# 340 dense tokens, 44 in two lanes beside the last 128, and row buffers that change roles

## The chip, the core and the metric

The kernel runs on one core of a Trainium2 chip. The time is the device time of one execution in microseconds (us), the median of the runs shown. TensorE is PE in the profile (its weight loads PEld), VectorE is DVE, ScalarE is ACT, GpSimd is POOL, SyncE is SP.

## What is computed

One decoder layer on 512 tokens of 2048 channels: RMS norm, a projection into a convolution group and an attention group, their output projection added to x, and then a channel mixer (PEER) on the normed result. The mixer is what the change is about:

```python
v1, i1 = lax.top_k(sub[:, :, 0], 16)          # 8 heads, 128 keys each half
v2, i2 = lax.top_k(sub[:, :, 1], 16)
vals, cidx = lax.top_k(v1[..., :, None] + v2[..., None, :] , 16)
experts = e1 * 128 + e2                        # 128 experts for each token
gates = softmax(vals)
h = einsum("cd,chkd->chk", xc, peer_u[experts])
a = gelu(h) * gates
y = einsum("chk,chkd->cd", a, peer_v[experts])
```

There are 16384 experts, each a row of 2048 floats in `peer_u` and in `peer_v`; each token uses 128 of them.

## The kernel before

The tokens of the mixer are split in three.

- **Dense tokens**, the first `TD` = 352. All experts are run for them, and a gate that is zero for the experts not chosen is applied. `expert_tile` (L940 on) makes, for one tile of 128 experts, 48 matmuls over `TD` columns (L949, L951, L952: three products of the high and low parts of weights and tokens, 16 chunks of channels), with a Gelu behind it. `fold_group` (L987 on) makes for eight such tiles eight pieces of 48 matmuls of the same width (L998, L1000, L1001) and adds them to `acc` on DVE (L1008).
- **The last 128 tokens**, one a partition. For each of their 128 experts a row is fetched by an indirect load from POOL (L845, `gather`), and one DVE instruction multiplies and sums it (L861, first half, rows of `peer_u`) or adds it to the output rows (L878, second half, rows of `peer_v`).
- **The `NB` = 32 tokens between**, in `LANES` = 4 lanes on the same 128 partitions: each lane does a quarter of a token's experts, so `SB` = 32 further steps in each half. The four partial sums of a token are added by a matmul at the end (`yo`, L1056).

So there are `STEPS` = 2 x (128 + 32) = 320 gather steps. In the first half steps 0 to 127 are of the last tokens and 128 to 159 of the lanes, and so again in the second half. Step n is one indirect load and one DVE instruction of 2048 elements a partition. The loads go in turn to two buffers `grow` and to a third, the row tile that the half does not use (`yrow` in the first, `xrow` in the second). A buffer is free again when the DVE instruction that reads it has ended.

The weights come from SP as one load for two units (8 KB a partition); ACT makes the rounded high part `w_hi` (L152), DVE the rest `w_lo` (L153); three buffers of each let them run ahead of PE.

Order. The program issues 256 ticks of 48 matmuls: 72 of `expert_tile` (groups 0 to 8, gelu values written to DRAM), then for groups 9 to 15 eight of `expert_tile` and eight of `fold_group`, then 72 of `fold_group`. `step` (L933 on) counts them and asks for gather steps by this rule:

```python
if tick[0] > START:
    gather_until(int((tick[0] - START) * STEPS / (END - START)) + 1, first)
```

Other DVE and ACT work (the decoding of the choices, `dense_gates` for `GT` = 16 tokens a chunk with its PE matmuls at L921) stands in a queue from which each tick takes some (`pump`). The framework then sets the final order of each engine by its own estimate of times, and each engine runs its list in order; what waits on one engine holds all behind it there. Three times a row tile is loaded anew when its step is reached: `xrow` at step 128, `yrow` at 160 and again at 288.

Of the kernel before, what the change touches and what calls it, by code (L numbers as in the profile page):

```python
# [9 lines left out]
FT = mybir.dt.float32  # L10
# [50 lines left out]
def hymba_layer(ctx: ExitStack, tc: tile.TileContext, xT, pos, par, row, wi, wo, wq, sk, ut, un, vt, vn,  # L61
                out_t, out_r, dbg=None):
    nc = tc.nc
# [107 lines left out]
    ident = const.tile([128, 128], FT, name="ident")  # L171
# [82 lines left out]
    for c in range(KC):  # L254
        if c % 4 == 0:
# [5 lines left out]
                                       op1=OP.subtract)  # L261
# [48 lines left out]
    at = ctx.enter_context(ExitStack())  # L310
# [225 lines left out]
    gat = ctx.enter_context(tc.tile_pool(name="gat", bufs=1))  # L536
# [298 lines left out]
    h3 = gat.tile([128, 128 + SB], FT, name="h3")  # L835
    rows = {"x": xrow, "y": None}
    STEPS = 2 * (128 + SB)

    def gather(src, k, after):
        if done[0] % 3 < 2:  # L840
            g = pu.tile([128, D], FT, name="grow", bufs=2)
        else:
            g = gat.tile([128, D], FT, name="yrow" if src is un else "xrow", bufs=1)
        at = idx[:, k:k + 1] if k < 128 else idxb[:, k - 128:k - 127]
        i = nc.gpsimd.indirect_dma_start(out=g, out_offset=None, in_=src,  # L845
                                         in_offset=bass.IndirectOffsetOnAxis(ap=at, axis=0))
        if after is not None:
            tc.add_manual_dep(i.ins, after.ins.name,
                              mybir.DependencyInfo(mybir.DependencyClass.NoSync, mybir.DependencyReason.DATA),
                              reason="spreads the gathers over the dense sweep")  # L850
        return g

    def gather_step(n, after):
        k = n % (128 + SB)
        if n < 128 + SB:
            if k == 128:
                rows["x"] = gat.tile([128, D], FT, name="xrow", bufs=1)
                for l in range(LANES):
                    nc.scalar.dma_start(rows["x"][l * NB:l * NB + NB], XB)
            g = gather(un, k, after)  # L860
            nc.vector.scalar_tensor_tensor(g, g, 1.0, rows["x"], op0=OP.mult, op1=OP.mult, accum_out=h3[:, k:k + 1])  # L861
            if k % 16 == 15:
                s = slice(k - 15, k + 1)
                w = GA3[:, s] if k < 128 else GB3[:, k - 143:k - 127]
                nc.scalar.activation(h3[:, s], h3[:, s], AF.Gelu)
                nc.vector.tensor_tensor(h3[:, s], h3[:, s], w, op=OP.mult)
        else:
            if k == 0:
                rows["y"] = gat.tile([128, D], FT, name="yrow", bufs=1)
                nc.scalar.dma_start(rows["y"], YA)  # L870
            if k == 128:
                nc.scalar.dma_start(out_r[NB:], rows["y"])
                rows["y"] = gat.tile([128, D], FT, name="yrow", bufs=1)
                nc.gpsimd.memset(rows["y"], 0.0)
                nc.scalar.dma_start(rows["y"][:NB], YB)
            y = rows["y"]
# [238 lines left out]
```

## Time and profile before

| | us |
|---|---|
| median of 3 runs | 2865.03 |
| runs, lowest to highest | 2859.58 to 2870.8 |
| the profiled execution, its own time | 2866.89 |
| its span, first to last instruction | 2864.8 |
| mean granted TensorE clock | 0.99 of full |

The profile is one execution; times in it count from the start of its span. Busy time is the time in which an engine has an instruction running; matmuls overlap, so PE's rate is read from the starts of successive matmuls. In the timeline the number behind the start is the duration, and a bracket holds the idle time before it with what ended it.

### The profile page before, as it was taken

The numbers are of one execution on the slowest core, as the hardware profiler recorded it, in microseconds if no ns is written. First come the engines' busy times: TensorE is split into PE (matmuls) and PEld (weight loads), VectorE is DVE, ScalarE is ACT, GpSimd is POOL, SyncE is SP. The second block draws the span as 40 slices with busy tenths as digits, with TensorE's granted clock in tenths as the row PEclk, the third lists the DMA queues.
The fourth block names the chain that finished last, engine by engine and source line by source line (L and its number), as shares of the span: only waits on it lengthen the run. The fifth ranks groups of instructions, "written<-read, shape, count | busy, mean of one in ns | idle before, by whom it ended". The sixth has DMA issues, their size and how long they took to land.

```text
span 2864.8 us, 42910 instructions
## 1 busy us (share of the span) xinstructions
PE 2812.4 (98%) x16995; PEld 2693.1 (94%) x16995; DVE 2369.8 (83%) x3586; ACT 1210.9 (42%) x1879; POOL 460.1 (16%) x337
## 2 busy tenths in 40 slices
PE   8999999999999999999999999999999999999996
PEld 8998877788899999999999999999999999999995
DVE  7888996569999888878688878788888888888796
ACT  5566434343343777666333332333323333333321
POOL 0000000000002122212221222222222112222232
PEclk9999999999999999999999999999999999999998
DMA  5222322433249989999989889899898988888796
GB/s 175 74 67 75 117 91 82 165 112 136 89 153 342 325 312 354 326 340 344 357 346 345 339 323 352 336 334 339 324 345 329 354 333 336 346 317 337 278 377 240
DMA packets 167337, 763.94 MB, mean 267 GB/s; under 512 B 14496, under 2 KB 66848, under 8 KB 90784
## 3 DMA queue, kind: packets, MB, share of 16 engines
q1 hardware_dynamic: 66720, 378.64, 35.7%
q0 software_dynamic: 46080, 335.56, 31.4%
q10 hardware_dynamic: 54336, 47.00, 4.9%
q8 instruction: 133, 2.18, 0.3%
q14 instruction: 68, 0.56, 0.1%
HBM read 716.42 MB, written 44.70 MB: 266 GB/s over the span
## 4 chain that ended last, share of the span: by engine, by line
PE 95%; DVE 2%; DMA 2%; issue 1%; ACT 1%; POOL 0%; POOLq 0%; ACTq 0%; DVEq 0%
PE mm L951 11%; PE mm L949 11%; PE mm L952 11%; PE mm L1000 11%; PE mm L998 11%; PE mm L1001 11%; PE gps L921 3%; PE mm L599 2%; PE mm L600 2%; PE mm L816 2%; PE mm L818 2%; PE mm L817 2%; PE mm L511 2%; PE mm L510 2%; PE mm L509 2%; PE mm L598 2%
## 5 line engine op out<-in xcount | busy, mean ns | idle before, releaser
L152 ACT ACTIVATE w_hi<-w_raw 128x1024 fp32r<-128x1024 f32 x628 | 664.5, 1059 | 1266.7 <-PE mm L1000 618.2
L153 DVE TENSOR_TENSOR w_lo<-w_raw,w_hi 128x1024 fp32r<-128x1024 f32 x628 | 766.8, 1224 | 310.9 <-ACT w_hi L152 307.7
L951 PE MATMUL mm<-nl,w_hi 128*128 128x352 f32 x2048 | 667.5, 326 | 0.0
L949 PE MATMUL mm<-nh,w_hi 128*128 128x352 f32 x2048 | 665.8, 325 | 1.0 <-ACT w_hi L152 1.0
L952 PE MATMUL mm<-nh,w_lo 128*128 128x352 f32 x2048 | 663.5, 325 | 0.0
L1000 PE MATMUL mm<-al,w_hi 128*128 128x352 f32 x2048 | 661.3, 323 | 0.0
L998 PE MATMUL mm<-ah,w_hi 128*128 128x352 f32 x2048 | 658.7, 323 | 1.7 <-DVE acc L1008 1.7
L1001 PE MATMUL mm<-ah,w_lo 128*128 128x352 f32 x2048 | 650.0, 323 | 2.0 <-DVE w_lo L153 1.9
L998 PEld LDWEIGHTS mm<-ah,w_hi 128*128 128x128 f32 x2048 | 384.7, 188 | 2.6 <-DVE acc L1008 2.6
L949 PEld LDWEIGHTS mm<-nh,w_hi 128*128 128x128 f32 x2048 | 384.6, 188 | 1.5 <-ACT w_hi L152 1.3
L1001 PEld LDWEIGHTS mm<-ah,w_lo 128*128 128x128 f32 x2048 | 383.3, 188 | 2.6 <-DVE w_lo L153 2.6
L1000 PEld LDWEIGHTS mm<-al,w_hi 128*128 128x128 f32 x2048 | 385.3, 188 | 0.0
L952 PEld LDWEIGHTS mm<-nh,w_lo 128*128 128x128 f32 x2048 | 385.0, 188 | 0.0
L951 PEld LDWEIGHTS mm<-nl,w_hi 128*128 128x128 f32 x2048 | 384.9, 188 | 0.2
L845 POOL DMA_INDIRECT grow<-un,idx x86 | 122.0, 1419 | 889.0 <-DVE grow L861 577.7
L878 DVE SCALAR_TENSOR_TENSOR yrow<-grow,h,yrow 128x2048 f32<-128x2048 f32 x107 | 251.1, 2347 | 7.3 <-DMA grow<-vn,idxb 7.3
L861 DVE SCALAR_TENSOR_TENSOR grow<-grow,xrow 128x2048 f32<-128x2048 f32 x107 | 244.2, 2284 | 3.5 <-DMA grow<-un,idxb 3.5
L845 POOL DMA_INDIRECT grow<-vn,idx x85 | 117.4, 1381 | 453.1 <-DVE yrow L878 439.0
L306 DVE SCALAR_TENSOR_TENSOR mix_c<-h,par,mix_c 128x512 f32<-128x512 f32 x240 | 173.7, 748 | 1.6
L1008 DVE TENSOR_TENSOR acc<-acc,mm 128x352 f32<-128x352 f32 x240 | 116.9, 517 | 56.4 <-PE mm L1001 56.1
L878 DVE SCALAR_TENSOR_TENSOR yrow<-xrow,h,yrow 128x2048 f32<-128x2048 f32 x53 | 124.4, 2347 | 0.1
L861 DVE SCALAR_TENSOR_TENSOR yrow<-yrow,xrow 128x2048 f32<-128x2048 f32 x53 | 121.1, 2285 | 1.0 <-DMA xrow<-XB 1.0
(274 smaller groups left out, 3889.5 us busy)
## 6 DMA issues: line engine op xcount, KB each, us to landing
w_raw<-ut SPq DMA_DIRECT2D x128, 1024.0 KB
w_raw<-vt SPq DMA_DIRECT2D x128, 1024.0 KB
w_raw<-wi SPq DMA_DIRECT2D x52, 512.0 KB
G<-gt ACTq DMA_DIRECT2D x22, 1024.0 KB
Gb<-G SPq DMA_DIRECT2D x16, 1408.0 KB
w_raw<-wo SPq DMA_DIRECT2D x32, 512.0 KB
w_raw<-wq SPq DMA_DIRECT2D x32, 512.0 KB
H<-gl ACTq DMA_DIRECT2D x18, 704.0 KB
```

Source lines behind the costliest of these rows:

```text
L152: nc.scalar.activation(hi, raw, AF.Copy)
L153: nc.vector.tensor_tensor(lo, raw, hi.bitcast(FT), op=OP.subtract)
L306: nc.vector.scalar_tensor_tensor(mix_c[:, c], h[:, k:k + T], w, mix_c[:, c], op0=OP.mult, op1=OP.add)
L845: i = nc.gpsimd.indirect_dma_start(out=g, out_offset=None, in_=src, in_offset=bass.IndirectOffsetOnAxis(ap=at, axis=0))
L861: nc.vector.scalar_tensor_tensor(g, g, 1.0, rows["x"], op0=OP.mult, op1=OP.mult, accum_out=h3[:, k:k + 1])
L878: nc.vector.scalar_tensor_tensor(y, g, h3[:, k:k + 1], y, op0=OP.mult, op1=OP.add)
L949: m = nc.tensor.matmul(bank, hi[:, s], nh[:, k, :TD], start=k == 0, stop=False)
L951: nc.tensor.matmul(bank, hi[:, s], nl[:, k, :TD], start=False, stop=False)
L952: nc.tensor.matmul(bank, lo[:, s], nh[:, k, :TD], start=False, stop=k == KC - 1)
L998: m = nc.tensor.matmul(banks[j], hi[:, ws], ah[:, ee], start=ee == 0, stop=False)
L1000: nc.tensor.matmul(banks[j], hi[:, ws], al[:, ee], start=False, stop=False)
L1001: nc.tensor.matmul(banks[j], lo[:, ws], ah[:, ee], start=False, stop=ee == 7)
```

## The change

`TD` becomes 340 and `NB` 44. There are two lanes in place of four, so a lane step covers `PB` = 88 partitions, and there are `SB` = 64 of them in each half: `STEPS` = 2 x (128 + 64) = 384. Gate chunks hold 20 tokens in place of 16 (17 chunks in place of 22, and 85 calls of `dense_gates` in place of 88). `START` and `END` go from 10 and 250 to 2 and 249. The row tile for the next stretch is loaded three steps ahead into the buffer that was the third gather buffer; then the two names change roles. The closing matmul has 44 output rows.

```diff
-TD = 352
+TD = 340
 TA = T - 128
 NB = TA - TD
-LANES = 128 // NB
+LANES = 2
+PB = LANES * NB
 SB = 128 // LANES
-GT = 16
+GT = 20
 AHEAD = 9
-START = 10
-END = 250.0
+START = 2
+END = 249.0
...
+    def load_rows(n):
+        t = gat.tile([128, D], FT, name=home[1], bufs=1)
+        if n == 128 + SB:
+            nc.scalar.dma_start(t, YA)
+        elif n == 128:
+            for l in range(LANES):
+                nc.scalar.dma_start(t[l * NB:l * NB + NB], XB)
+        else:
+            nc.gpsimd.memset(t, 0.0)
+            nc.scalar.dma_start(t[:NB], YB)
+        spare[n] = t
...
-        if done[0] % 3 < 2:
+        if done[0] % 3 < 2 or spare:
             g = pu.tile([128, D], FT, name="grow", bufs=2)
         else:
-            g = gat.tile([128, D], FT, name="yrow" if src is un else "xrow", bufs=1)
-        at = idx[:, k:k + 1] if k < 128 else idxb[:, k - 128:k - 127]
+            g = gat.tile([128, D], FT, name=home[1], bufs=1)
+        at = idx[:, k:k + 1] if k < 128 else idxb[:PB, k - 128:k - 127]
+        g = g[:128 if k < 128 else PB]
...
+        if n + 3 in SWITCH:
+            load_rows(n + 3)
+        if n in spare:
+            if n == SWITCH[2]:
+                nc.scalar.dma_start(out_r[NB:], rows["y"])
+            rows["x" if n == 128 else "y"] = spare.pop(n)
+            home.reverse()
...
-        nc.tensor.matmul(ps, fold_s.rearrange("p l n -> p (l n)"), rows["y"][:, cs], start=True, stop=True)
+        nc.tensor.matmul(ps[:NB], fold_s, rows["y"][:, cs], start=True, stop=True)
```

How the built programs stand. First DVE in the stretch of the lane steps of the first half, near tick 102: `w_lo` is one per 24 matmuls, the instruction with `x2048` is a gather step. Before:

```order
L153 TENSOR_TENSOR w_lo<-w_raw,w_hi 128x1024 x2
L861 SCALAR_TENSOR_TENSOR grow,h_7303<-grow,xrow 128x2048
L1008 TENSOR_TENSOR acc<-acc,mm 128x352 x2
L861 SCALAR_TENSOR_TENSOR grow,h_7303<-grow,xrow 128x2048
L153 TENSOR_TENSOR w_lo<-w_raw,w_hi 128x1024 x2
L861 SCALAR_TENSOR_TENSOR yrow,h_7303<-yrow,xrow 128x2048
L1008 TENSOR_TENSOR acc<-acc,mm 128x352 x2
```

Now:

```order
L154 TENSOR_TENSOR w_lo<-w_raw,w_hi 128x1024
L884 SCALAR_TENSOR_TENSOR xrow,h_7303<-xrow,yrow 88x2048
L154 TENSOR_TENSOR w_lo<-w_raw,w_hi 128x1024
L884 SCALAR_TENSOR_TENSOR grow,h_7303<-grow,yrow 88x2048
L1024 TENSOR_TENSOR acc<-acc,mm 128x340 x2
L154 TENSOR_TENSOR w_lo<-w_raw,w_hi 128x1024
L890 TENSOR_TENSOR h_7303<-h_7303,GB_5224 88x16
L884 SCALAR_TENSOR_TENSOR grow,h_7303<-grow,yrow 88x2048
L154 TENSOR_TENSOR w_lo<-w_raw,w_hi 128x1024
L884 SCALAR_TENSOR_TENSOR xrow,h_7303<-xrow,yrow 88x2048
L1024 TENSOR_TENSOR acc<-acc,mm 128x340 x2
```

Before there are three gather steps for two ticks in this place; now each `w_lo` has a step behind it, two for each tick. Over ticks 80 to 119 DVE's list holds 54 gather steps before and 78 now. Over ticks 0 to 23 it holds 18 before and 32 now, with 9 fewer of the decoding instructions on `dec_oh` (L770 to L774) and 4 fewer `oh` of the gates, which stand later. In the other stretches up to tick 247 eight ticks hold 8 to 13 steps now and 6 to 13 before.

Then the end of DVE's list, from one of the last `w_lo` on. The two `acc` rows come after the last matmuls of `fold_group`. Before:

```order
L153 TENSOR_TENSOR w_lo<-w_raw,w_hi 128x1024
L878 SCALAR_TENSOR_TENSOR yrow<-grow,h_7303,yrow 128x2048
L153 TENSOR_TENSOR w_lo<-w_raw,w_hi 128x1024
L878 SCALAR_TENSOR_TENSOR yrow<-xrow,h_7303,yrow 128x2048
L1008 TENSOR_TENSOR acc<-acc,mm 128x352 x2
L878 SCALAR_TENSOR_TENSOR yrow<-grow,h_7303,yrow 128x2048
L1008 TENSOR_TENSOR acc<-acc,mm 128x352 x2
L878 SCALAR_TENSOR_TENSOR yrow<-grow,h_7303,yrow 128x2048
L878 SCALAR_TENSOR_TENSOR yrow<-xrow,h_7303,yrow 128x2048
L878 SCALAR_TENSOR_TENSOR yrow<-grow,h_7303,yrow 128x2048 x2
L878 SCALAR_TENSOR_TENSOR yrow<-xrow,h_7303,yrow 128x2048
L878 SCALAR_TENSOR_TENSOR yrow<-grow,h_7303,yrow 128x2048 x2
```

Now, up to the fifth step behind the last `acc`:

```order
L154 TENSOR_TENSOR w_lo<-w_raw,w_hi 128x1024
L894 SCALAR_TENSOR_TENSOR yrow<-grow,h_7303,yrow 88x2048
L154 TENSOR_TENSOR w_lo<-w_raw,w_hi 128x1024
L1024 TENSOR_TENSOR acc<-acc,mm 128x340 x2
L894 SCALAR_TENSOR_TENSOR yrow<-grow,h_7303,yrow 88x2048
L894 SCALAR_TENSOR_TENSOR yrow<-xrow,h_7303,yrow 88x2048
L1024 TENSOR_TENSOR acc<-acc,mm 128x340 x2
L894 SCALAR_TENSOR_TENSOR yrow<-grow,h_7303,yrow 88x2048 x2
L894 SCALAR_TENSOR_TENSOR yrow<-xrow,h_7303,yrow 88x2048
L894 SCALAR_TENSOR_TENSOR yrow<-grow,h_7303,yrow 88x2048 x2
L894 SCALAR_TENSOR_TENSOR yrow<-xrow,h_7303,yrow 88x2048
```

Behind the last `acc` stand 7 gather steps before. Now the pattern of the last three rows goes on to the end of the list: 30 steps, all of 88 partitions, with nothing else between them; the loads on POOL stand in the same order.

## Rows read from the trace of the kernel before

**Rows 1.** the page, parts 1, 3 and 4: busy time, DMA queues, the chain.

```profile
PE 2812.4 (98%) x16995; PEld 2693.1 (94%) x16995; DVE 2369.8 (83%) x3586; ACT 1210.9 (42%) x1879; POOL 460.1 (16%) x337
...
q0 software_dynamic: 46080, 335.56, 31.4%
...
PE 95%; DVE 2%; DMA 2%; issue 1%; ACT 1%; POOL 0%; POOLq 0%; ACTq 0%; DVEq 0%
```

**Rows 2.** busy time by stretch (us, PE, PEld, DVE, ACT, POOL, clock, DMA share, GB/s).

```profile
764.00:957.00 193.00, 192.01 (x1191) 189.61 (x1190) 183.67 (x480) 81.56 (x112) 26.57 (x18) 1.00 0.66 242
1600.00:1800.00 200.00, 200.00 (x1252) 200.00 (x1251) 162.22 (x176) 62.94 (x73) 46.96 (x35) 1.00 0.91 339
2400.00:2600.00 200.00, 200.00 (x1247) 200.00 (x1246) 174.20 (x190) 66.92 (x84) 44.53 (x29) 1.00 0.87 339
2215.00:2225.00 10.00, 10.00 (x65) 10.00 (x64) 5.89 (x7) 2.97 (x3) 0.98 (x1) 1.00 1.01 427
```

**Rows 3.** timeline of PE: first and last matmul of runs at 256, 512 columns, and gates (start, us).

```profile
201.40 0.28 PE L327 MATMUL mm<-w_hi,xh 128*128 128x256 f32 x1
...
202.72 0.28 PE L330 MATMUL mm<-w_hi,xl 128*128 128x256 f32 x1
...
699.76 0.40 PE L817 MATMUL mm<-nl,w_hi 128*128 128x512 f32 x1
...
703.03 0.39 PE L816 MATMUL mm<-nh,w_hi 128*128 128x512 f32 x1
...
951.52 1.95 PE L921 MATMUL gps<-og,oh 128*128 128x128 f32 x16
953.23 0.41 PE L949 MATMUL mm<-nh,w_hi 128*128 128x352 f32 x1
```

**Rows 4.** the page, part 5: weight loads of one dense line (count, busy, mean ns).

```profile
L998 PEld LDWEIGHTS mm<-ah,w_hi 128*128 128x128 f32 x2048 | 384.7, 188 | 2.6 <-DVE acc L1008 2.6
```

**Rows 5.** timeline of DVE near 1600 us: one gather step between its neighbours.

```profile
1599.26 2.29 DVE L861 SCALAR_TENSOR_TENSOR grow<-grow,xrow 128x2048 f32<-128x2048 f32 x1
1601.47 0.08 DVE L861 DVE_READ_ACCUMULATOR grow<-grow,xrow 128x1 f32 x1
1601.47 0.52 DVE L188 TENSOR_TENSOR al<-hv,ah 128x352 fp32r<-128x352 f32 x1
1601.90 1.22 DVE L153 TENSOR_TENSOR w_lo<-w_raw,w_hi 128x1024 fp32r<-128x1024 f32 x1
1603.04 2.29 DVE L861 SCALAR_TENSOR_TENSOR yrow<-yrow,xrow 128x2048 f32<-128x2048 f32 x1
```

**Rows 6.** groups of DVE instructions by line, 764 to 957 us (count, busy, mean ns, idle).

```profile
L153 DVE TENSOR_TENSOR w_lo<-w_raw,w_hi 128x1024 fp32r<-128x1024 f32 x49 | 60.0, 1225 | 8.4 <-ACT w_hi L152 7.6 <-issue 0.7
...
L772 DVE TENSOR_TENSOR dec_oh<-dec_oh,iif 128x1024 f32<-128x1024 f32 x10 | 12.3, 1225 | 0.0
...
L914 DVE TENSOR_TENSOR oh<-iof,kt 128x1024 f32<-128x1024 f32 x4 | 4.7, 1218 | 0.0
```

**Rows 7.** timeline: the first dense w_lo on DVE, the first sweep matmul on PE.

```profile
763.57 1.25 DVE L153 TENSOR_TENSOR w_lo<-w_raw,w_hi 128x1024 fp32r<-128x1024 f32 x1
...
772.73 0.33 PE L949 MATMUL mm<-nh,w_hi 128*128 128x352 f32 x1
```

**Rows 8.** timeline of DVE, 2737 to 2773 us: first and last of nine gather steps.

```profile
2737.09 2.35 DVE L878 SCALAR_TENSOR_TENSOR yrow<-grow,h,yrow 128x2048 f32<-128x2048 f32 x1
...
2772.47 2.35 DVE L878 SCALAR_TENSOR_TENSOR yrow<-xrow,h,yrow 128x2048 f32<-128x2048 f32 x1
```

**Rows 9.** timeline of the end: PE's last dense matmul, DVE's steps, the closing matmul.

```profile
2831.04 0.32 PE L1001 MATMUL mm<-ah,w_lo 128*128 128x352 f32 x1
...
2831.84 2.35 DVE L878 SCALAR_TENSOR_TENSOR yrow<-grow,h,yrow 128x2048 f32<-128x2048 f32 x1
2834.22 2.35 DVE L878 SCALAR_TENSOR_TENSOR yrow<-xrow,h,yrow 128x2048 f32<-128x2048 f32 x1
2836.61 2.35 DVE L878 SCALAR_TENSOR_TENSOR yrow<-grow,h,yrow 128x2048 f32<-128x2048 f32 x1
2841.96 2.35 DVE L878 SCALAR_TENSOR_TENSOR yrow<-grow,h,yrow 128x2048 f32<-128x2048 f32 x1 [3.00 <-DMA grow<-vn,idxb]
2844.39 2.35 DVE L878 SCALAR_TENSOR_TENSOR yrow<-xrow,h,yrow 128x2048 f32<-128x2048 f32 x1
2847.61 2.35 DVE L878 SCALAR_TENSOR_TENSOR yrow<-grow,h,yrow 128x2048 f32<-128x2048 f32 x1 [0.87 <-DMA grow<-vn,idxb]
2852.20 2.35 DVE L878 SCALAR_TENSOR_TENSOR yrow<-grow,h,yrow 128x2048 f32<-128x2048 f32 x1 [2.24 <-DMA grow<-vn,idxb]
...
2854.61 2.07 PE L1056 MATMUL yo<-yrow,fold_s 128*128 128x512 f32 x2 [23.25 <-DVE yrow L878]
```

**Rows 10.** timeline of POOL in that stretch: issues of indirect loads.

```profile
2834.45 2.93 POOL L845 DMA_INDIRECT grow<-vn,idxb  x1 [5.83 <-DVE yrow L878]
2837.69 2.08 POOL L845 DMA_INDIRECT xrow<-vn,idxb  x1 [0.30 <-issue]
2840.08 0.94 POOL L845 DMA_INDIRECT grow<-vn,idxb  x1 [0.31 <-issue]
2844.58 2.97 POOL L845 DMA_INDIRECT grow<-vn,idxb  x1 [3.56 <-DVE yrow L878]
```

**Rows 11.** the chain of waits, 2830 us to the end: from an issue to its landing.

```profile
2834.45 7.41 DMA grow<-vn,idxb
...
2844.58 7.53 DMA grow<-vn,idxb
```

More of the change, by code (lines that the diff above doesn't have):

```diff
@@ L667, in hymba_layer @@
             xb = xtp.tile([128, 512], FT, name="xb", bufs=1)
-            nc.scalar.activation(xb[128 - NB:], src[128 - NB:], AF.Copy)
+            nc.scalar.activation(xb[64:], src[64:], AF.Copy)
             nc.scalar.dma_start(to[:, c4 * 512:c4 * 512 + 512], xb[128 - NB:])
@@ L792, in lane_lists @@
     def lane_lists():
-        ps_ = slice(128 - NB, 128)
+        ps_ = slice(64, 128)
         ib = kp.tile([128, 128], I32, name="ib")
@@ L796, in lane_lists @@
         e2 = E2[ps_, 2].rearrange("p h k -> p (h k)")
-        ga = GA[ps_, 2].rearrange("p h k -> p (h k)")
+        ga = GA[128 - NB:, 2].rearrange("p h k -> p (h k)")
         nc.vector.scalar_tensor_tensor(ib[ps_], e1, 128.0, e2, op0=OP.mult, op1=OP.add)
         for l in range(LANES):
-            nc.scalar.dma_start(idxb[l * NB:l * NB + NB], ib[ps_, l * SB:l * SB + SB])
+            nc.scalar.dma_start(idxb[l * NB:l * NB + NB], ib[128 - NB:, l * SB:l * SB + SB])
             nc.scalar.dma_start(GB3[l * NB:l * NB + NB], ga[:, l * SB:l * SB + SB])
@@ L834, in hymba_layer @@
     pu = ctx.enter_context(tc.tile_pool(name="pu", bufs=1))
-    h3 = gat.tile([128, 128 + SB], FT, name="h3")
+    h3 = pu.tile([128, 128 + SB], FT, name="h3")
     rows = {"x": xrow, "y": None}
     STEPS = 2 * (128 + SB)
+    home = ["xrow", "yrow"]
+    spare = {}
+    def load_rows(n):
[9 more added lines that the diff above has]
+        spare[n] = t
     def gather(src, k, after):
-        if done[0] % 3 < 2:
+        if done[0] % 3 < 2 or spare:
             g = pu.tile([128, D], FT, name="grow", bufs=2)
         else:
-            g = gat.tile([128, D], FT, name="yrow" if src is un else "xrow", bufs=1)
-        at = idx[:, k:k + 1] if k < 128 else idxb[:, k - 128:k - 127]
+            g = gat.tile([128, D], FT, name=home[1], bufs=1)
+        at = idx[:, k:k + 1] if k < 128 else idxb[:PB, k - 128:k - 127]
+        g = g[:128 if k < 128 else PB]
         i = nc.gpsimd.indirect_dma_start(out=g, out_offset=None, in_=src,
@@ L851, in gather @@
         return g
+    SWITCH = (128, 128 + SB, 256 + SB)
     def gather_step(n, after):
         k = n % (128 + SB)
+        if n + 3 in SWITCH:
[5 more added lines that the diff above has]
+            home.reverse()
+        p = 128 if k < 128 else PB
         if n < 128 + SB:
[L856 to L859, printed above, removed]
             g = gather(un, k, after)
-            nc.vector.scalar_tensor_tensor(g, g, 1.0, rows["x"], op0=OP.mult, op1=OP.mult, accum_out=h3[:, k:k + 1])
+            nc.vector.scalar_tensor_tensor(g, g, 1.0, rows["x"][:p], op0=OP.mult, op1=OP.mult,
+                                           accum_out=h3[:p, k:k + 1])
             if k % 16 == 15:
                 s = slice(k - 15, k + 1)
-                w = GA3[:, s] if k < 128 else GB3[:, k - 143:k - 127]
-                nc.scalar.activation(h3[:, s], h3[:, s], AF.Gelu)
-                nc.vector.tensor_tensor(h3[:, s], h3[:, s], w, op=OP.mult)
-        else:
[L868 to L876, printed above, removed]
+                w = GA3[:, s] if k < 128 else GB3[:PB, k - 143:k - 127]
+                nc.scalar.activation(h3[:p, s], h3[:p, s], AF.Gelu)
+                nc.vector.tensor_tensor(h3[:p, s], h3[:p, s], w, op=OP.mult)
+        else:
+            y = rows["y"][:p]
             g = gather(vn, k, after)
-            nc.vector.scalar_tensor_tensor(y, g, h3[:, k:k + 1], y, op0=OP.mult, op1=OP.add)
+            nc.vector.scalar_tensor_tensor(y, g, h3[:p, k:k + 1], y, op0=OP.mult, op1=OP.add)
     done = [0]
@@ L1045, in hymba_layer @@
     gather_until(STEPS, None)
-    fold_s = mg.tile([128, LANES, NB], FT, name="fold_s")
-    nc.vector.tensor_copy(fold_s[:, 0], ident[:, 0:NB])
+    fold_s = mg.tile([128, NB], FT, name="fold_s")
+    nc.vector.tensor_copy(fold_s, ident[:, 0:NB])
     for l in range(1, LANES):
-        nc.vector.tensor_tensor(fold_s[:, 0], fold_s[:, 0], ident[:, l * NB:l * NB + NB], op=OP.add)
-    for l in range(1, LANES):
-        nc.vector.tensor_copy(fold_s[:, l], fold_s[:, 0])
+        nc.vector.tensor_tensor(fold_s, fold_s, ident[:, l * NB:l * NB + NB], op=OP.add)
     yo = pu.tile([128, D], FT, name="grow", bufs=2)
```

## The prediction

> **What bounds the kernel now.** I read the page first: PE is busy for 98% of the span and makes 95% of the chain of waits [rows 1]. So nearly all time is a count of matmuls times their spacing. The stretches say it more finely: in the 200 us from 1600 us on PE starts 1252 matmuls at the full clock and is never idle, while DVE is busy for 162 us and the DMA engines for 0.91 [rows 2]. One dense matmul of 352 columns thus costs 200 / 1252 = 159.7 ns. Two other things must be kept in mind: DVE is close behind PE (184 of 193 us at the start of the sweep, 174 of 200 late in the folds [rows 2]), and after the last dense matmul PE stops and the rest is a tail of gather steps, 2831.4 to 2854.6 us, with 10 us of closing work behind it [rows 9]. The change makes PE's part shorter, gives DVE more, and alters the tail, so each is priced by itself.
>
> **Matmuls of 340 columns.** There are 12288 of them (256 ticks of 48). Spacing at other widths shows what a column costs: at 256 columns 11 starts take 1.32 us, 120 ns each; at 512 columns 14 starts take 3.27 us, 233.6 ns each [rows 3]. From 256 to 352 that is 39.7 ns for 96 columns, 0.41 ns each; from 352 to 512 it is 73.9 for 160, 0.46 each. Twelve columns fewer save 5.0 to 5.5 ns; I take 5.25, so 12288 x 5.25 ns = 64.5 us (61 to 68). The new spacing is 154.4 ns. [...]
>
> **Gates.** Three calls of `dense_gates` fewer are 24 matmul records fewer; 16 of them take 1.71 us from their first start to the next dense one [rows 3], so 24 save 2.6 us. ACT and DVE work of these calls is beside PE and counts nothing.
>
> **The start of the sweep.** DVE's list has 14 more gather steps in the first 24 ticks, 9 fewer on `dec_oh` and 4 fewer `oh`. A step takes 2.21 us to the next instruction's start [rows 5], so +31 us; the others 1.22 us each [rows 6], less some overlap, so -15. DVE was busy for 184 of 193 us there [rows 2] and would need 200, where PE needs 24 x 48 x 154.4 ns = 178 in place of 184. DVE starts 9 us ahead of PE [rows 7], so PE waits for some 22 - 9 = 13 us, against a few before. I take 11 us more (4 to 20).
>
> **The lane steps of the first half.** Ticks 80 to 119 hold 78 steps, where it were 54. In these 40 ticks DVE has 80 `w_lo` at 1.14 us from start to start, 78 steps at 2.21 and 80 small ones (`hv`, `al` or `acc`) at 0.43 [rows 5]: 91 + 172 + 34 = 298 us; PE needs 40 x 48 x 154.4 ns = 296.5. DVE is thus as long as PE, with no room for what it waits for. Nothing, if it packs perfectly; the other end is the pace of steps beside the dense stream late in the kernel, eight in 35.4 us or 4.42 each [rows 8], which for 78 is 345 us, 48 too many, though with loads of 128 rows and not 88. I take 6 us. Elsewhere the list holds 8 to 13 steps for eight ticks, much as before, and DVE keeps its room; I cost the full-width steps there at nothing, hidden behind PE. If that cover went, each late step would hold the `w_lo` behind it.
>
> **The switches.** Three loads of row tiles go out three steps earlier; the chain before holds none of them, so I count nothing. During the three steps the third gather buffer is missing, six to nine steps in all, beside PE. [...]
>
> **The tail.** This term decides. DVE runs its list in order, and behind the last `acc`, which waits for the last matmul, stand 30 steps where it were 7. Before, the 7 took 23.2 us, from 2831.4 to 2854.6 [rows 9]: three found their rows landed and ran 2.39 us apart, then each buffer went round in 10.1 to 10.2 us (2831.84 to 2841.96 to 2852.20), so three steps in 10.2, 3.4 each. The round can be followed [rows 9 to 11]: the step ends; POOL issues the next load into its buffer, 2.93 us because DVE is at the next step meanwhile (0.94 us where DVE was idle); the load lands 7.4 us after the issue began; the step of 2.35 us. With rows of 88 partitions DVE's step is as long (2048 elements a partition). Only the load may shrink: 320 loads hold 31.4% of the 16 engines' span [rows 1], 2.81 us each, of which 40 of 128 rows are 0.88. A round is then 9.3 us, 3.1 a step. If all three loads were always in time, DVE alone would set 2.39; if a load of 88 rows takes as long as one of 128, 3.4. No row shows how 88 rows spread, so I take 3.2, nearest to the measured round: 30 x 3.2 = 96 us, 73 more than before (49 at 2.39, 79 at 3.4). The closing work is as before.
>
> **Sum.** On the profiled execution, 2866.9: -64.5 - 2.6 + 11 + 6 + 73 = 2889.8. That execution is 1.9 above the median, so I forecast 2888 us: slower by 0.8%. The columns gain what was to be gained, and the tail gives back a little more than that. 0.5% is about what a measurement of this kernel can tell from no change.
>
> **Rivals.**
>
> - *The load of 88 rows is no shorter than one of 128.* [...] No run here shows a gather of 88. As a mechanism: the round stays 10.2 us, a step 3.4, the tail 102 us, the time 2894. It would show as loads of the same time from first issue to landing. Against it stands nothing in the rows. Chance 0.18.
> - *No change.* The tail at 3.0 (90 us, +67) and DVE keeping up at the start and in the lanes: 2866.9 - 67 + 67 - 1.9 = 2865. For it: DVE has idle time in most stretches and PE's stalls were few. Against it: the sums for DVE above exceed PE's. Values from 2851 to 2879 fall here. Chance 0.25.
> - *Faster: DVE sets the tail.* If POOL's issues fall into gaps of DVE (0.94 us in place of 2.93, 2 us less a round) and 88 rows land 0.9 us sooner, a round is 7.3 us and the steps come 2.4 us apart, 72 us in all, +49. With 68 us from the columns and no new stalls: 2866.9 - 68 - 2.6 + 49 - 1.9 = 2843. It decides from a round below 7.2 us on, three DVE steps. Against it: the three issues that met a step took 2.08 to 2.97 us, and only the one made while DVE was idle took 0.94 [rows 10]. Chance 0.10.
> - *Slower by more: lane steps hold PE.* If the 78 steps run at 4.42 us, 48 us in place of 6: 2930. For it: beside the dense stream the loads were only just in time [rows 8]; against it: fewer bytes a load. Chance 0.10.
> - *The columns don't count, since weight loads set the spacing.* A load shows 188 ns [rows 4], more than the spacing. Then nothing is gained and the time is 2952. Against it: with the same loads 256 columns go at 120 ns [rows 3]. Chance 0.03.
>
> DMA engines as the bound: 64 more steps of 88 rows but two lanes mean 256 x 1.05 + 128 x 0.72 = 361 MB of gathers in place of 336; 22 of it falls in the tail. The dense part, 3% shorter, would move some 350 GB/s, below the 427 that ten microseconds show [rows 2]. I hold this in the range, not as a case.
>
> **How the numbers follow.** The forecast has 0.34 and lies from 2880 to 2905 by its bounds. With the first rival (0.18), the lanes (0.10) and the weight loads (0.03) slower by over 0.5%, above 2879, has 0.65; no change 0.25; faster 0.10. The range takes the upper half of the no-change case and part of the lanes' rival: 2856 to 2914, leaving out about 0.1 on either side.
>
> **What would show it.** Dense matmuls 154 to 155 ns apart. The last dense matmul near 2781 us (2831 - 67 + 17). Thirty steps behind it, 9.3 to 10.2 us a round, POOL issues near 3 us where they meet a step. DVE near 100% at 800 to 950 us and in ticks 80 to 119, with PE idle there for 10 to 25 us. I am wrong if the tail's steps come 2.4 us apart, if PE shows no idle time before the tail, or if the spacing stays at 160 ns.

## The result and the profile after

The change made the kernel slower: 3117.38 us (median of 4 runs, 3110.0 to 3120.02) beside 2865.04 us before (4 runs, 2859.58 to 2870.8), a ratio of 1.0877 with a 95% interval of 1.0853 to 1.0901. The forecast was 2888 us, with a range up to 2914: the sign was right, the size was 23 us in place of 252.

The page of the changed kernel, parts 1, 3 and 4, beside [rows 1]:

```profile
PE 2801.1 (90%) x16971; PEld 2664.7 (85%) x16971; DVE 2501.7 (80%) x3676; ACT 1211.0 (39%) x1866; POOL 618.3 (20%) x401
...
q0 software_dynamic: 55296, 360.76, 36.1%
q1 hardware_dynamic: 66727, 377.41, 35.1%
...
PE 67%; issue 14%; DMA 9%; DVE 6%; POOL 3%; ACT 1%; POOLq 0%; DVEq 0%
```

PE was the bound before (95% of the chain of waits); now it makes 67%. The gather queue q0 moves 7.5% more bytes, and its packets take 36.1% x 3116.7 = 1125 us of the 16 engines where it were 31.4% x 2864.8 = 900, 25% more. The weights, on q1, moved the same bytes within 0.4% and took 1094 us where it were 1023 (35.7% of the span before).

Busy time by stretch in the changed kernel (columns as in [rows 2]):

```profile
764.00:957.00 193.00, 185.85 (x1186) 182.76 (x1185) 191.39 (x435) 73.76 (x91) 53.14 (x33) 1.00 0.85 320
...
1600.00:1800.00 200.00, 140.76 (x768) 135.85 (x768) 124.32 (x131) 40.60 (x50) 62.05 (x32) 0.85 0.95 212
2000.00:2200.00 200.00, 200.00 (x1294) 200.00 (x1293) 165.71 (x142) 69.64 (x84) 41.59 (x35) 1.00 0.88 335
2400.00:2600.00 200.00, 198.43 (x1279) 197.87 (x1278) 176.52 (x194) 65.21 (x78) 50.52 (x30) 1.00 0.90 343
```

Where the loads fetch 128 rows (2000 to 2200 us) all is as forecast: PE never idle, 200 / 1294 = 154.6 ns from matmul to matmul, 335 GB/s with the DMA engines 0.88 busy. In the lane stretch (1600 to 1800 us) PE starts 768 matmuls in place of some 1290, DVE is less busy than elsewhere, and the DMA engines are 0.95 busy but move only 212 GB/s. Neither PE nor DVE is the limit there; the engines that carry the loads are full and slow.

The timeline of DVE in that stretch of the changed kernel shows how this reaches PE:

```profile
1655.32 2.29 DVE L884 SCALAR_TENSOR_TENSOR xrow<-xrow,yrow 88x2048 f32<-88x2048 f32 x1 [2.37 <-DMA xrow<-un,idxb]
...
1657.54 1.22 DVE L154 TENSOR_TENSOR w_lo<-w_raw,w_hi 128x1024 fp32r<-128x1024 f32 x1
1667.08 2.29 DVE L884 SCALAR_TENSOR_TENSOR grow<-grow,yrow 88x2048 f32<-88x2048 f32 x1 [8.32 <-DMA grow<-un,idxb]
```

A lane step waits 8.32 us for its load, and everything behind it on DVE waits too: the next `acc` and `w_lo`, and behind these PE. The groups of waits of the changed kernel (us in total, times, longest):

```profile
DVE grow L884 <- DMA grow<-un,idxb: 94.3, 31, 8.3
DVE yrow L894 <- DMA grow<-vn,idxb: 76.0, 30, 6.0
...
PE mm L1017 <- DVE w_lo L154: 60.0, 27, 6.6
PE mm L968 <- DVE w_lo L154: 43.4, 17, 7.4
PE mm L1014 <- DVE acc L1024: 33.9, 11, 6.7
```

Before, the corresponding waits for lane loads came to 3.5 us (first half) and 7.3 us (second half).

The tail of the changed kernel (timeline of all engines), beside [rows 9 to 11]:

```profile
2979.89 2.35 DVE L894 SCALAR_TENSOR_TENSOR yrow<-xrow,h,yrow 88x2048 f32<-88x2048 f32 x1 [5.86 <-DMA xrow<-vn,idxb]
...
2982.53 0.96 POOL L862 DMA_INDIRECT xrow<-vn,idxb  x1 [6.38 <-DVE yrow L894]
...
2990.43 2.35 DVE L894 SCALAR_TENSOR_TENSOR yrow<-xrow,h,yrow 88x2048 f32<-88x2048 f32 x1 [0.29 <-DMA xrow<-vn,idxb]
...
3102.92 2.35 DVE L894 SCALAR_TENSOR_TENSOR yrow<-xrow,h,yrow 88x2048 f32<-88x2048 f32 x1 [0.79 <-DMA xrow<-vn,idxb]
...
3105.37 6.05 PE L1070 MATMUL yo<-yrow,fold_s 128*44 128x512 f32 x8 [129.64 <-issue]
```

31 steps stand between the last dense matmul and the end, 2979.89 to 3102.92: 4.10 us a step, where the forecast took 3.2 and allowed 3.4. (The first of them stands ahead of the last `acc` in DVE's list, so the 30 of the forecast are the others.) The load issued at 2982.53 landed 7.9 us later although its issue took only 0.96; before, 7.41 us held an issue of 2.93 [rows 10, 11]. Behind the issue this load takes 6.9 us, where the one before took 4.5.

### The profile page after: what moved, and what is told of

It reads as the page before. It is cut to its first block, busy times and chain, and to the rows that moved or that the text cites. A ratio compares the mean times of both kernels' runs of the same rounds, so it can differ in the third digit from the quotient of the medians.

```text
span 3116.7 us, 43134 instructions
## 1 busy us (share of the span) xinstructions
PE 2801.1 (90%) x16971; PEld 2664.7 (85%) x16971; DVE 2501.7 (80%) x3676; ACT 1211.0 (39%) x1866; POOL 618.3 (20%) x401
## 3 DMA queue, kind: packets, MB, share of 16 engines
q0 software_dynamic: 55296, 360.76, 36.1%
## 4 chain that ended last, share of the span: by engine, by line
PE 67%; issue 14%; DMA 9%; DVE 6%; POOL 3%; ACT 1%; POOLq 0%; DVEq 0%
PE mm L965 7%; PE mm L968 7%; PE mm L967 7%; PE mm L1017 6%; PE mm L1014 6%; PE mm L1016 6%; DMA grow<-vn,idxb 3%; PE gps L937 2%; POOL grow L862 2%; PE mm L600 2%; PE mm L817 2%; PE mm L512 2%; PE mm L511 2%; PE mm L818 2%; PE mm L819 2%
## 5 line engine op out<-in xcount | busy, mean ns | idle before, releaser
L1017 PE MATMUL mm<-ah,w_lo 128*128 128x340 f32 x2048 | 647.9, 326 | 60.0 <-DVE w_lo L154 60.0
L968 PE MATMUL mm<-nh,w_lo 128*128 128x340 f32 x2048 | 655.5, 322 | 43.5 <-DVE w_lo L154 43.4
L1014 PE MATMUL mm<-ah,w_hi 128*128 128x340 f32 x2048 | 661.6, 325 | 33.9 <-DVE acc L1024 33.9
L965 PE MATMUL mm<-nh,w_hi 128*128 128x340 f32 x2048 | 660.1, 322 | 14.5 <-DVE acc L1024 11.5
L1016 PE MATMUL mm<-al,w_hi 128*128 128x340 f32 x2048 | 660.8, 323 | 9.9 <-DVE al L189 9.9
L967 PE MATMUL mm<-nl,w_hi 128*128 128x340 f32 x2048 | 659.0, 322 | 0.0
L894 DVE SCALAR_TENSOR_TENSOR xrow<-grow,h,xrow 128x2048 f32<-128x2048 f32 x87 | 204.3, 2349 | 1.6 <-DMA grow<-vn,idx 1.6
L884 DVE SCALAR_TENSOR_TENSOR grow<-grow,yrow 88x2048 f32<-88x2048 f32 x43 | 98.3, 2286 | 94.5 <-DMA grow<-un,idxb 94.3
L894 DVE SCALAR_TENSOR_TENSOR yrow<-grow,h,yrow 88x2048 f32<-88x2048 f32 x42 | 98.6, 2347 | 76.1 <-DMA grow<-vn,idxb 76.0
L1024 DVE TENSOR_TENSOR acc<-acc,mm 128x340 f32<-128x340 f32 x240 | 113.3, 504 | 47.6 <-PE mm L1017 47.4
```

Source lines behind the costliest of these rows:

```text
L884: nc.vector.scalar_tensor_tensor(g, g, 1.0, rows["x"][:p], op0=OP.mult, op1=OP.mult, accum_out=h3[:p, k:k + 1])
L894: nc.vector.scalar_tensor_tensor(y, g, h3[:p, k:k + 1], y, op0=OP.mult, op1=OP.add)
L965: m = nc.tensor.matmul(bank, hi[:, s], nh[:, k, :TD], start=k == 0, stop=False)
L967: nc.tensor.matmul(bank, hi[:, s], nl[:, k, :TD], start=False, stop=False)
L968: nc.tensor.matmul(bank, lo[:, s], nh[:, k, :TD], start=False, stop=k == KC - 1)
L1014: m = nc.tensor.matmul(banks[j], hi[:, ws], ah[:, ee], start=ee == 0, stop=False)
```

## Where the 252 us are

The dense stream has 256 ticks of 48 matmuls, so the starts of certain matmuls (first of the stream, of ticks 80, 128 and 240, and the last) cut every run into the same stretches. Timeline of PE before (first and last are in [rows 7, 9]):

```profile
1471.43 0.32 PE L998 MATMUL mm<-ah,w_hi 128*128 128x352 f32 x1
...
1842.34 0.33 PE L998 MATMUL mm<-ah,w_hi 128*128 128x352 f32 x1
...
2707.97 0.33 PE L998 MATMUL mm<-ah,w_hi 128*128 128x352 f32 x1
```

The same of the changed kernel:

```profile
764.83 0.32 PE L965 MATMUL mm<-nh,w_hi 128*128 128x340 f32 x1
...
1447.23 0.32 PE L1014 MATMUL mm<-ah,w_hi 128*128 128x340 f32 x1
...
1964.48 0.32 PE L1014 MATMUL mm<-ah,w_hi 128*128 128x340 f32 x1
...
2810.93 0.32 PE L1014 MATMUL mm<-ah,w_hi 128*128 128x340 f32 x1
...
2975.41 0.31 PE L1017 MATMUL mm<-ah,w_lo 128*128 128x340 f32 x1
```

And of the run `e9_after_64_mid` (below), which is the changed kernel with other lane loads:

```profile
769.07 0.32 PE L969 MATMUL mm<-nh,w_hi 128*128 128x340 f32 x1
...
1453.12 0.32 PE L1018 MATMUL mm<-ah,w_hi 128*128 128x340 f32 x1
...
1845.69 0.32 PE L1018 MATMUL mm<-ah,w_hi 128*128 128x340 f32 x1
...
2691.38 0.32 PE L1018 MATMUL mm<-ah,w_hi 128*128 128x340 f32 x1
...
2810.33 0.31 PE L1021 MATMUL mm<-ah,w_lo 128*128 128x340 f32 x1
```

Fewer columns take 48 x (159.74 - 154.56) ns = 0.249 us off a tick, 63.7 us in all. What is left of the differences to before, with that taken out by itself:

| stretch | after, us | e9, us | forecast, us |
|---|---|---|---|
| up to the first dense matmul | -7.9 | -3.7 | 0 |
| 12 columns fewer, all ticks | -63.7 | -63.7 | -64.5 |
| ticks 0 to 79 (start of the sweep, gates) | +3.6 | +5.3 | +8.4 |
| ticks 80 to 127 (lanes, first half) | +158.3 | +33.6 | +6 |
| ticks 128 to 239 | +8.7 | +7.9 | 0 |
| ticks 240 to 255 (lanes, second half) | +45.4 | -0.1 | 0 |
| behind the last dense matmul | +107.5 | +59.1 | +73 |
| sum, against the span of 2864.8 | +251.9 | +38.4 | +22.9 |

So little was lost where the gathers have 128 rows (at most 8.7 us in a stretch, and 7.9 of it in e9 too). Nearly all of the surprise lies in the three stretches with loads of 88 rows.

## The experiments

Runs e1 to e6, e9 and e10 are single executions; the others have five or six.

**Is it the loads, and what about them?** The first four runs shared a chip, on which the kernel before took 2862.49 us. The theories then: the number of rows decides (88 does not divide over 16 engines as 80, 96 and 128 do); the pace of 192 steps in a half is too high whatever the rows; any load that covers a part of the 128 partitions is slow.

`e1_rows96`: the changed kernel, lane loads of 96 rows (8 of them unused).

```diff
+GP = 96
...
-        at = idx[:, k:k + 1] if k < 128 else idxb[:PB, k - 128:k - 127]
+        at = idx[:, k:k + 1] if k < 128 else idxb[:GP, k - 128:k - 127]
```

> The changed kernel, but each lane load fetches 96 rows into 96 partitions (the eight extra rows are row 0 of the table and are not used); DVE still works on 88. Theory 'row count': the loads of 88 rows are slow because 88 is not a multiple of 16, so they go over fewer DMA engines; with 96 a load costs about 2.1 us of the 16 engines (96/128 of 2.81), PE stalls in ticks 80 to 127 fall from 160 us to under 40, and the time is 2880 to 2930. Rival 'pace': two steps a tick are too many for three buffers whatever the load; ticks 80 to 127 stay over 480 us and the time is 3080 to 3150. Rival 'any part of 128': every load of fewer than 128 partitions is slow; time as with 88 or above, 3100 to 3200.

Measured 3029.29 us. Busy time by stretch:

```profile
1600.00:1800.00 200.00, 159.79 (x962) 155.28 (x962) 141.66 (x154) 49.69 (x60) 55.37 (x35) 0.94 1.01 258
```

Still full at 258 GB/s, with PE idle for a fifth of the stretch: 96 rows are faster than 88 but far from the rate of 128. The time lies in the range of none of the three theories.

`e2_rows128`: the same with `GP = 128` (40 rows unused).

> The changed kernel, but each lane load fetches 128 rows (40 unused). Theory 'row count' and rival 'any part of 128': a load costs 2.81 us of the 16 engines, lane steps run no slower than full ones; DVE's list holds 55 steps behind the last acc, so the time is 2780 + 55 x 3.4 + 10 = 2950 to 2990, below the 3117 of the change in spite of more bytes. Rival 'pace': lane steps as slow as with 88 rows or slower, over 3117.

Measured 3000.76 us. Busy time by stretch:

```profile
1600.00:1800.00 200.00, 200.00 (x1292) 200.00 (x1291) 164.24 (x181) 66.40 (x78) 59.70 (x35) 1.00 0.88 336
```

The same lanes, buffers and columns, and a third more bytes a load than with 96 rows, yet PE is not idle in the stretch and the engines move 336 GB/s at 0.88. This does not settle the question of the pace, for the framework's order is another one here: in ticks 88 to 127 DVE runs 53 gather steps, as many as in the kernel before (54), where the changed kernel runs 74. (Ticks 80 to 127 are still 24 us longer by the count of the table above, 22 of them in the first eight ticks, where 18 steps fall, all of full width. The changed kernel loses 13 us in the same eight ticks, so that part of its loss is not of the loads of 88 rows. What holds PE there was not tested; a Gelu on ACT waits 9.3 us for a gather step, and the next `w_hi` stand behind it.) The steps that are left over, 55 of them, stand behind the last dense fold; from the step ahead of them on they ran 3.40 us apart (2798.14 to 2984.93 in the timeline), which is the step of before [rows 9] and costs 190 us. The time is 11 us beyond what was expected.

`e3_rows80`: loads of 80 rows; the experts of the last 8 rows of the second lane are left out.

```diff
-PB = LANES * NB
+PB = 80
```

> The changed kernel with lane steps of 80 rows; the last 8 rows' experts (of lane 1) are left out. 80 is a multiple of 16. Theory 'row count': loads cost about 1.8 us of the 16 engines, ticks 80 to 127 nearly free of stalls, 28 steps behind the last acc at about 3: 2860 to 2910. Rival 'any part of 128' and rival 'pace': over 3050.

Measured 2973.22 us; q0 takes 35.6% for 352.35 MB, and PE starts 972 matmuls from 1600 to 1800 us. 80 and 96 rows both divide by 16 and both are slow, so the theory of the number of rows can't be all of it. It is not out either: this time too lies between the ranges of the theories, and 88 rows are the slowest of the three, with 768 matmuls in that stretch beside 962 and 972.

`e4_before_88`: the kernel before, its lane loads and lane steps cut to 88 rows; the experts of the other 40 rows are left out.

```diff
+GP = 88
...
-        at = idx[:, k:k + 1] if k < 128 else idxb[:, k - 128:k - 127]
+        at = idx[:, k:k + 1] if k < 128 else idxb[:GP, k - 128:k - 127]
+        g = g[:128 if k < 128 else GP]
```

> The kernel before with its lane steps on 88 of the 128 partitions; the experts of the other 40 rows of the lanes are left out. 64 of 320 loads are of 88 rows, at the old pace (1.3 steps a tick). Theory 'row count': each of these costs over 3 us of the 16 engines although it holds 0.72 MB, so queue 0 takes at least as large a share as before (31.4%) for 315 MB; loads arrive late in the lane stretches and the time is 2870 to 2930. Rival 'pace': a load costs 1.93 us, queue 0 falls to 29.5%, and the time is 2840 to 2860 (two steps behind the last acc in place of seven).

Measured 2928.33 us, 66 us slower than the kernel before with 31% of the lane bytes taken away. Busy time by stretch:

```profile
1710.00:1880.00 170.00, 151.55 (x893) 150.09 (x894) 116.94 (x126) 45.66 (x57) 41.20 (x25) 0.92 1.00 226
```

So it needs nothing else of the change: old columns, old pace, old buffers, and loads of 88 rows fill the engines at 226 GB/s. This run, and e9 below at the new pace, speak against the pace as the main cause; e2 does not.

**Part of the partitions, or which part?** Three theories: what a row costs hangs on which of the 128 partitions a load reaches ("places"); any load of fewer than 128 partitions is slow ("part"); 64 rows are as cheap as in a full load ("neither"). The next two runs fetch the same 64 rows and differ in the place alone, partitions 0 to 63 and 32 to 95. That these two places differ was my guess; no run up to here shows it. Both are the kernel before; the vector work of a lane step takes 32 of the rows, the others are left out.

`e5_before_64_low`: partitions 0 to 63. (The next run: `G0, G1 = 32, 96` and `V0, V1 = 64, 96`.)

```diff
+G0, G1 = 0, 64
+V0, V1 = 0, 32
...
-        at = idx[:, k:k + 1] if k < 128 else idxb[:, k - 128:k - 127]
+        at = idx[:, k:k + 1] if k < 128 else idxb[:G1 - G0, k - 128:k - 127]
+        g = g if k < 128 else g[G0:G1]
```

> The kernel before, whose lane loads fetch 64 rows instead of 128, onto partitions 0 to 63; the vector work of a lane step takes 32 of them, so the experts of the other rows of the lanes are left out. [...] Theory 'neither' (64 rows as cheap as in a full load): share 0.68 at 250 GB/s, 1252 matmuls, 2835 to 2865.

Measured 2863.39 us. The page, part 3, and the lane stretch of the windows:

```profile
q0 software_dynamic: 41984, 302.01, 30.3%
```

```profile
1710.00:1880.00 170.00, 169.49 (x1059) 169.06 (x1058) 137.19 (x148) 55.34 (x69) 41.00 (x28) 1.00 0.99 270
```

`e6_before_64_mid`: partitions 32 to 95.

> As the run before it, but the 64 rows lie on partitions 32 to 95 (the index list is the same 64 indices); the same rows in number and bytes, the same work left out. [...] Theory 'part': slow as in the run on partitions 0 to 63, share 0.90 or more, fewer than 1240 matmuls, 2865 to 2930.

Measured 2842.04 us. The same two rows:

```profile
q0 software_dynamic: 41984, 302.01, 28.9%
```

```profile
1710.00:1880.00 170.00, 170.00 (x1065) 170.00 (x1065) 141.17 (x147) 54.90 (x67) 43.66 (x29) 1.00 0.77 270
```

The same bytes at the same 270 GB/s hold the engines 0.99 of the time on partitions 0 to 63, and 0.77 on 32 to 95. At equal rows, the place decided here what a load cost. (From 1600 to 1800 us, the stretch that the numbers of "part" and "neither" are for, half of the loads are still full ones: 0.95 and 0.79 at 277 GB/s, with 1246 and 1250 matmuls. "Part" is out: e6 is under its share and its time. The low run has a share far over the 0.68 of "neither", but its time lies in the range of "neither", 1.6 us under the upper end, and it lost less than I had estimated for "places". The engines were full, but just kept up; it is the share beside that of e6 that speaks for the place.)

What a lane load costs follows from q0. A full load takes 31.4% x 2864.8 us / 320 = 2.81 us of the 16 engines; 256 full loads make 719.6, and the rest of each run's q0 time, divided by its lane loads, gives:

| lane load | run | us of 16 engines | ns a row | tail, us a step |
|---|---|---|---|---|
| 128 rows | before | 2.81 | 22 | 3.39 |
| 128 rows | e2 | 2.79 | 22 | 3.40 |
| 88 rows, 0 to 87 | after; e4 | 3.17; 3.20 | 36 | 4.10 (after) |
| 96 rows, 0 to 95 | e1 | 3.06 | 32 | 3.25 |
| 80 rows, 0 to 79 | e3 | 2.64 | 33 | 3.19 |
| 64 rows, 0 to 63 | e5; e10 | 2.30; 2.25 | 36; 35 | 3.16 (e10) |
| 64 rows, 32 to 95 | e6; e9 | 1.58; 1.50 | 25; 23 | 2.90 (e9) |

A load of 88 rows on partitions 0 to 87 costs more than one of 128. The last column (steps behind the last dense matmul, from start to start) shows that the place is not all of it: the 35 steps of e1, with eight rows more in much the same place, ran 3.25 us apart.

```profile
2903.11 2.35 DVE L897 SCALAR_TENSOR_TENSOR yrow<-grow,h,yrow 88x2048 f32<-88x2048 f32 x1 [0.59 <-DMA grow<-vn,idxb]
...
3013.47 2.35 DVE L897 SCALAR_TENSOR_TENSOR yrow<-xrow,h,yrow 88x2048 f32<-88x2048 f32 x1 [0.84 <-DMA xrow<-vn,idxb]
```

What sets 88 apart can be counted in the traces. Queue q0 holds 144 packets for a load of 88 rows, 56 of them of 4 bytes; a load of 64, 80, 96 or 128 rows has 16 of these. In the tail of the changed kernel (2990 to 3100 us) 11 packets of 8 KB are in flight at once for 26% of the time and 16 for 27%; in the tail of e1 (2910 to 3010 us) it is 16 for 64%, and 11 for less than 3%. So fewer rows of a load are on the way at a time, and each takes longer: 585 ns on the mean of that tail, where it took 360 in the tail before (2836 to 2850 us). (88 is 11 x 8; that these are eleven engines with eight rows each is my reading, for the trace names no engine.)

**Does it explain the change?** If "places" holds, the stalls go with the loads of e6, though everything else stays. `e9_after_64_mid` keeps all of the change (columns, 192 steps in a half, ticks 2 to 249, roles of the buffers) and puts 64 rows on partitions 32 to 95 (the edit of e6, with `V0, V1 = 64, 88`); the vector work takes 24 of the rows, the others are left out.

> The changed kernel as it stands (340 dense columns, 192 steps in each half, tick 2 to 249), with lane loads of 64 rows on partitions 32 to 95 in place of 88 on 0 to 87; the vector work of a lane step takes 24 of them, the experts of the other rows are left out. 28 steps behind the last dense fold. [...] Rival (the columns, the pace or the buffers of the change stall the lane steps whatever the loads are): blocks over 65 us, last dense matmul after 2840, over 2920.

Measured 2905.02 us (before, on that chip, 2864.73). Its stretches stand in the table above; the lane stretch of the windows:

```profile
1600.00:1800.00 200.00, 191.93 (x1196) 187.63 (x1195) 197.19 (x205) 60.25 (x72) 81.34 (x50) 0.98 0.75 275
```

212 of the 252 us are gone, with as many steps in ticks 88 to 127 (74) as in the changed kernel. The stretch did not become free, though: PE is held back by 33.6 us in ticks 80 to 127. Some 15 of them fall in the first eight ticks, where the loads are full ones; in the lane stretch behind, DVE is busy for 197 of 200 us. The rival is out by its time (2905 for over 2920) and by the last dense matmul (2810 for after 2840), but blocks of eight ticks took 59 to 68 us, the first 77, so not all are under its 65; 8 x 48 matmuls at 154.6 ns are 59.4. The time is also 5 us beyond the 2870 to 2900 that I had estimated for "places", around the forecast of 2888. The tail of e9, timeline of DVE:

```profile
2811.22 2.34 DVE L898 SCALAR_TENSOR_TENSOR yrow<-xrow,h,yrow 24x2048 f32<-24x2048 f32 x1
...
2889.65 2.34 DVE L898 SCALAR_TENSOR_TENSOR yrow<-xrow,h,yrow 24x2048 f32<-24x2048 f32 x1
```

28 steps, 2.90 us each. These loads carry 64 rows and not 88, so e9 is kinder to the DMA engines than any true version of the change would be, and it is still 40 us slower than before.

`e10_after_64_low`: the same on partitions 0 to 63 (`V0, V1 = 0, 24`).

> As the run before it, the 64 rows on partitions 0 to 63. Theory 'places': slower than the run before it, with the DMA engines over 0.95 busy in the lane stretch at under 290 GB/s, blocks of 8 ticks of 60 to 68 us there, tail 2.8 to 3.6 us per step, time 2890 to 2950. Theory 'rows' (a short load is slow or fast by its number of rows alone): the same time as the run before it within 5 us.

Measured 2957.47 us, 52 us more than e9 by the place of the rows alone. Its lane stretch:

```profile
1600.00:1800.00 200.00, 176.99 (x1063) 170.33 (x1064) 171.06 (x186) 53.80 (x64) 87.52 (x45) 0.97 0.92 246
```

Direction and place as expected by "places", 7 us beyond the upper end; the engines were 0.92 busy where 0.95 was expected, and blocks of eight ticks took 65 to 77 us where 60 to 68 were.

So of the 212 us, 52 are the place at equal rows. The other 160 lie between the 64 rows of e10 and the 88 of the change, with 16 and 56 small packets a load; no run takes the bytes and the split apart there. But e1, with more bytes than the change and sixteen packets in flight for 64% of its tail, is 88 us faster than it (with 69 steps in ticks 88 to 127 for 74), so I give the split of 88 rows, eleven at a time, a good part in it.

**What is the rest of the change worth?** `e7_order_alone` is the changed kernel with the old columns and lanes.

```diff
-TD = 340
+TD = 352
...
-LANES = 2
+LANES = 4
...
-GT = 20
+GT = 16
```

> The change with 352 dense columns, four lanes of 32 rows and chunks of 16 as before: what is left of it is the start at tick 2, the end at 249 and the roles of the row buffers. Its order has 2 steps behind the last dense fold, before has 7. My theory (the loads of 88 rows cost the time, the order does not): no stall in the lane stretches, 5 steps fewer in the tail are -17 us at 3.4, the early start costs about +11, so 2850 to 2866. Rival 'order' (the early start or the switches of the buffers hold the lane steps up): over 2900.

Measured 2850.01 us, 0.9952 (0.9938 to 0.9966) of the kernel before: faster, as the theory had it, and no stall in the lanes.

`e8_order_start10_end246`: the same with `START = 10` and `END = 246.0`.

> As the run before it, with the start back at tick 10 and the end at 246, again 2 steps behind the last dense fold. My theory: the first three blocks of eight ticks return to 59 to 62 us and the tail stays short, 2840 to 2855, under the kernel before. Rival: the steps that no longer run early push the pace up and matmuls wait for w_lo in the sweep, so no better than the run that starts at tick 2.

Measured 2856.13 us, 0.9971 (0.9959 to 0.9983). My expectation missed and the rival held: it is no better than the start at tick 2. What is won by the short tail is in part given back in the sweep.

`e11_before_start2_end249`: the kernel before, where only the two numbers change.

```diff
-START = 10
-END = 250.0
+START = 2
+END = 249.0
```

> The kernel before with the steps from tick 2 to 249 and nothing else: the buffers keep their roles. 2 steps behind the last dense fold. If the earlier start gives what the run of the order alone gained (ratio 0.9952), this gives it too, 2847 to 2855. If the roles of the buffers gave it (no wait for the reload of a row buffer at the switches), this stays at 2858 to 2867.

Measured 2853.38 us, 0.9954 (0.994 to 0.9967): as much as e7. So the ticks give the gain, and the roles of the row buffers give nothing that can be measured.

`e12_order_end247`: e7 with `END = 247.0`.

> The run of the order alone (352 columns, four lanes of 32 rows on all 128 partitions, start at tick 2) with the end at 247 in place of 249: no step stands behind the last dense fold, where that run has 2 and the kernel before 7. If the tail is all that the order changes, 2 steps at 3.4 us less: 2841 to 2848, ratio about 0.993. Rival: the steps taken out of the tail hold the last folds by as much, 2849 to 2856, ratio about 0.996.

Measured 2847.33 us, 0.9939 (0.9925 to 0.9952). Its interval overlaps that of e7, so the two bounds of the expectation are not told apart; of the runs that leave no experts out it is the fastest.

## Why the prediction was right in sign and wrong in size

- **Columns: right.** 154.6 ns from start to start where 154.4 was forecast; 63.7 us in place of 64.5. The rival that weight loads set the spacing is out.
- **Start of the sweep and gates: right in place, too dear.** +3.6 us for +8.4. DVE was at 191 of 193 us there, as the sum had it. The 7.9 us by which the first dense matmul came earlier stood in no term.
- **The tail: the step that failed.** "Only the load may shrink", 40 of 128 rows being 0.88 us, and 3.4 us a step as the upper bound "if a load of 88 rows takes as long as one of 128". That a load of fewer rows could cost more than a full one was not among the cases. It cost 3.17 us of the engines for 2.81, the step 4.10 for 3.2. The steps took 123 us (2979.89 to 3102.92) where 96 were forecast; of the rest of 107.5 against 73, 3.7 us are the first step, which started 4.5 us behind the last matmul, 0.8 before [rows 9], and 2.4 the one step more. The first rival, a load of 88 rows no shorter than one of 128, was nearer, though no row of before showed a reason for it. But it priced the load as a full one and so ended at 3.4 as well; the rows took 585 ns each where it were 360, and 11 were in flight for 26% of the tail. In e1, with sixteen in flight for 64% of the tail, the rows are nearly as dear (32 ns for 36), and so they are in e3 (33), so the number in flight is not all that decides, but the tails of these two run at 3.25 and 3.19 us a step, as was forecast for 88. I take it that it needed both, dear rows and eleven at a time, to make the tail that long.
- **The lane steps of the first half: the same error, larger.** The prediction bounded them at 0 to 48 us by the pace of full loads, "though with loads of 128 rows and not 88", and took 6. They cost 158. With loads that cost a row what a full load does (e9, 23 ns for 22) the term is 33.6 us: inside the bounds, and the 6 was too near the end at which DVE packs perfectly. About half of it comes where DVE is at its limit, as the sum of 298 us against 296.5 had pointed out; the other half falls in ticks 80 to 87, where DVE is busy for 63 of 77 us.
- **"DMA engines as the bound", left out as a case.** The argument went by bytes: 350 GB/s needed, 427 seen in ten microseconds [rows 2]. It held for full loads (335 to 343 GB/s). In the lane stretch of the first half the engines were full at 212. This was the rival to have: one cause, dear loads, that acts in three stretches.
- **Ticks 240 to 255: forecast 0, came +45.** The same loads; in e9 the term is -0.1.
- **Switches: right at nothing**, as e7 beside e11 shows.

With the loads' fault taken away, e9 lands at 2905, inside the range, but with a lane term larger and a tail shorter than forecast. The change gives DVE 64 more steps of 2.3 us, 150 us of work on an engine that was 83% busy, for 64 us of PE: in this order it did not pay even with the cheapest loads that were run.

## What to carry to other kernels

Before a full-width load is cut to part of the partitions, price a row by the place it lands in and not by bytes; 64 rows on partitions 32 to 95 cost two thirds of 64 rows on 0 to 63 here, and 88 rows from partition 0 on cost more than 128. If a part of a load is not needed, compare with fetching all of it (with 40 useless rows in each load, e2 took 117 us less than the change, though in an order of its own), or with a number of rows that goes sixteen at a time (e1, 96 rows of which 8 are useless, sixteen in flight for 64% of its tail, took 88 us less). And where a price has no row in the trace, let its bound reach past the nearest row on both sides: "less work cannot take longer" is itself a claim about the hardware.

## What the runs showed of the hardware

- The place of the lane loads shows in the weights' queue too, which shares the 16 engines: it took 36.9% of the span in e5 and 36.3% in e6, 1056 us and 1031 for the same bytes (in the change, 1094 where it were 1023 before). In the change the DMA engines were 0.95 busy at 212 GB/s from 1600 to 1800 us and 0.88 at 335 from 2000 to 2200. The share alone does not tell; share beside GB/s does.
- 64 rows were cheaper on partitions 32 to 95 than on 0 to 63: the engines were 0.77 busy against 0.99 at the same 270 GB/s (e6, e5), and the cost of a load was about 1.5 times on the lower ones (2.25 to 2.30 us against 1.50 to 1.58). Why, and why a row on partitions 0 to 87 takes 1.6 times as long as in a full load (36 ns for 22), is left open: no run shows which engine writes which partition.
- Indirect loads of 88 rows had 11 packets of 8 KB in flight for 26% of the tail (under 3% in e1, with 96 rows), and 56 small packets a load in place of 16. The engines are 0.79 busy at 174 GB/s from 2990 to 3100 us there, and 0.97 at 246 in the tail of e1 (2910 to 3010 us).
- In the lane stretch the granted clock was 0.85 of full on the mean of 1600 to 1800 us, in which PE was idle for 59 of the 200 us. It was 1.00 from 2000 to 2200 us, with PE never idle, and 0.50 from 2990 to 3100 us, with no matmul.
